# Block products of a latent-attention input stage: order of the last two products, pace of the operands, one rotary step for all latent keys

## The chip, the cores and the metric

The kernel runs on one core of a Trainium2 chip. The core has five engines with a queue of instructions each: TensorE (PE in the profile; PEld is its weight load), VectorE (DVE), ScalarE (ACT), GpSimd (POOL) and SyncE (SP), which issues most DMAs. TensorE writes only to PSUM, which has eight banks of 128 x 512 float32 words; vector and scalar read it, GpSimd doesn't. The metric is the device time in microseconds of one execution. For several executions the median stands.

## The reference

Two layers of a backbone over 1024 latent tokens with 256 context tokens, width 1024. Layer 0 is windowed attention, layer 1 multi-head latent attention, each behind an adaptive normalisation. The change lies at the start of layer 1, where the normalised tokens are multiplied by one input matrix and the result is cut into four parts:

```python
def project(h):
    n = h.shape[1]
    cq, ckv, kr, g = jnp.split(h @ w_in, [B_Q_LORA, B_Q_LORA + B_KV_LORA, B_Q_LORA + B_KV_LORA + B_ROPE], axis=-1)
    q = (rms_norm(cq, q_norm) @ w_uq).reshape(b, n, B_HEADS, B_NOPE + B_ROPE)
    kv = (rms_norm(ckv, kv_norm) @ w_ukv).reshape(b, n, B_HEADS, B_NOPE + B_V)
    return q[..., :B_NOPE], q[..., B_NOPE:], kv[..., :B_NOPE], kr, kv[..., B_NOPE:], g
...
qrx = apply_rope(qrx, cos, sin)
krx = apply_rope(krx, cos, sin)
```

`cq` has 512 columns, `ckv` 256, `kr` 32 and `g` 1024. `ckv` and `kr` are needed for all 1280 tokens, `cq` and `g` for the 1024 latent ones. `kr` of the latent tokens is turned by a rotary step: it is multiplied by a cosine, its halves are swapped and multiplied by a signed sine, and the two are added.

## The kernel before

**Float32 by three products.** A float32 factor is cut into a high part (a cast by ScalarE, line 125) and a low part (what is left, a subtraction by VectorE or GpSimd, line 126); this is `split`. A product of two such factors is three matmuls, lines 130 to 132 (`mm3`). Nearly all matmuls of this stage have these three lines, whatever they belong to.

**The latent tiles.** `kv_tile` multiplies 128 tokens by the 288 columns of `ckv` and `kr` into one of three PSUM banks. It takes the norm of the first 256 columns (`rstd`: a square on ScalarE, line 1025, a scaling on VectorE, line 1026, a power on GpSimd, line 1027), scales them (line 1065) into a ring buffer `e`, and puts the last 32 columns into `krF`, a copy for the two context tiles and a rotary step (`rope`, lines 281, 286 and 291) for the eight latent ones. Two transposes (line 1078), a split and two stores of a tile are kept in a list `pend` and done by `flush` up to two tiles later. Ten tiles are done in the order `order1`. Between them the tokens of later tiles are normalised (`norm_x`, lines 231 to 234) and turned (`turn_h`, lines 245 to 254).

**The block products.** `cq` and `g` are computed by a scheme that makes a two by two block product of seven products instead of eight. The weights are six groups of 256 columns, two of kind `cq` and four of kind `g`; a group's weights are cut into four blocks (`raw(i, j)`), the tokens into two halves of the width and two halves of the sequence. `t_sums` makes the token side, T1 to T4, from sums and differences (lines 1093 to 1102), once for each half of the 512 token pairs. On the weight side `op(n)` makes the operand of product n: A11, A12, A22, and S1 to S4 with the sums in lines 1137, 1139, 1143 and 1151. Each operand is split into a slot of `wslot`, a ring of eight, with its low part on GpSimd. `fetch` loads a group's weights in two halves into a ring of two buffers (line 1118).

`P(n)` is a product of twelve 128 x 512 matmuls. A group has four PSUM banks d, c, a, b. P(1) and P(2) share d, P(6) uses c, P(5) uses b and P(7) uses a. P(4) adds to what P(7) left in a, and P(3) adds to what P(5) left in b. Before that, the result of P(5) or P(7) is read out of the bank by a vector addition (line 1177). The results of P(4) and P(3) are read in line 1185, and P(6)'s in line 1171. `post` then stores a block; for the kind `cq` it also sums squares (`sqacc`, lines 1201 to 1205), and for the kind `g` it applies a gate function (line 1192).

Products of one group run in the order of `todo`: 6, 5, 7, 4, 3, with P(1) and P(2) done ahead or in between. The operands come from one generator, `operands()`, which runs over all groups; after every product one `next(ops)` makes one operand, so that the operands stay eight ahead of the products, and the load of a group stands directly ahead of its first operand. `latent_rms` makes the factor of the `cq` norm from `sqacc`: sixteen small matmuls (line 1210), a scaling and a power (1214, 1215), eight transposes (line 1220) and two copies (line 1221).

**After the groups** `qr_tile` multiplies eight tiles by the rotary part of the query weights, applies `rope`, and leaves four transposes (line 1248) and two stores to `pend`; `flush(2)` does them two tiles later. Later `make_kr` reads `krF`.

Outside the part marked `manual_schedule`, a planner sets the order of the instructions on every engine: it goes by the order of the program and by when it takes an instruction's inputs to be ready. So matmuls of a tile and of a product can stand mixed on TensorE.

Of the kernel before, what the change touches and what calls it, by code (L numbers as in the profile page):

```python
# [60 lines left out]
def kernel(ctx: ExitStack, tc: tile.TileContext, t, out, dbg=None):  # L61
# [990 lines left out]
    def kv_tile(ti):  # L1052
# [13 lines left out]
        kr = krF[:, ti : ti + 1, :]  # L1066
        if ti < 2:
            nc.vector.tensor_copy(kr, shp(ps[:, 256:288], 1, 32))
        else:
            rope(  # L1070
                kr, shp(ps[:, 256:288], 1, 32), cosb[:, ti - 2, :], sinb[:, ti - 2, :], 1, 32,
                shp(e[:, 288:320], 1, 32),
            )
# [13 lines left out]
        pend.append(rest)  # L1087

# [18 lines left out]
    class Group:  # L1107

        def __init__(self, c0, kind, ch, banks):
            self.c0, self.kind, self.ch = c0, kind, ch  # L1110
            self.d, self.c, self.a, self.b = [PB[:, i, :] for i in banks]

        def fetch(self, n=2):
            self.w = []
            for h in range(2):
# [3 lines left out]
                self.w.append(w)  # L1119
# [87 lines left out]
    def latent_rms():  # L1207
# [8 lines left out]
        for h, bank in ((0, 6), (1, 7)):  # L1216
            pt = PB[:, bank, :]
            for i in range(4):
                r = rc[:, 4 * h + i : 4 * h + i + 1].to_broadcast([128, 128])
                nc.tensor.transpose(pt[:, i * 128 : i * 128 + 128], r, ident)  # L1220
            nc.scalar.copy(r_b[h], pt)
# [60 lines left out]
    rest5 = (6, 5, 7, 4, 3)  # L1282
    todo = [(0, (1, 2)), (1, (1, 2))] + [(i, rest5) for i in range(4)]
    todo += [(4, (1, 6, 5, 7, 2, 4, 3)), (5, (1, 6, 2, 5, 7, 4, 3))]

    def operands():
        for i, ns in todo:
            groups[i].fetch(len(ns) // 4 + 1 if len(ns) > 2 else 1)
            for n in ns:
                groups[i].op(n)  # L1290
                yield

    t_rest = []
    ops = operands()
    order1 = [2 * p + j for p in (0, 1, 3, 2, 4) for j in range(2)]
    nx = norm_x(src1(order1[4]), xr, junk)
    for i, ti in enumerate(order1):
# [9 lines left out]
        if i in (1, 5):  # L1307
            g = groups[2 + i // 4]
            g.d = PB[:, 3 + i // 4, :]
            g.fetch(1)  # L1310
# [11 lines left out]
        if i == 7:  # L1322
            t_rest.append(t_sums(xts[2], xts[4], slice(256, 512), xts[2][:, 4:8]))
        if i in (5, 7):
# [3 lines left out]
            if i == 7:  # L1328
                wslot.i = 0
                next(ops)  # L1330
                next(ops)
    flush()
    next(ops)
    next(ops)
    wr = Ring(F, [30, 26], 1024)
    for _ in range(4):
        next(ops)
        if t_rest:
            t_rest.pop(0)()
    for gi, ns in todo:  # L1340
        g = groups[gi]
        last = gi == 5
        for i, n in enumerate(ns):
            g.P(n)
            next(ops, None)
            if gi == 4 and i == 1:
                latent_rms()
# [564 lines left out]
```

## Time and profile before

| | us |
|---|---|
| median of 3 runs | 1595.35 (1591.12 to 1597.8) |
| the profiled execution | 1591.68 |
| its span, first to last instruction | 1590.0 |
| latent tiles begin (about) | 710 |
| block products, all but those among the latent tiles | 780.7 to 917.2 |
| eight query tiles and what follows | 917.2 to 985 |

The profile of the execution, its first two parts cut to the engines that matter here:

```profile
DVE  3878996657777777766633453667677677577354
ACT  4432222377777777768523433455555555545322
POOL 1151212136565555443554462588688688689410
PEclk9999999999999999998989999999999999999999
```

Each of the forty digits is a slice of 39.75 us and gives the busy share in tenths (9 is 90% or more); PEclk is the clock that was granted to TensorE, in tenths of full speed. The stage of the block products runs from slice 20 to the start of slice 24, counted from 1. A wait in a profile's list names the engine and line that waited, what released it, the total in us, the number of times and the longest. A row of the timeline gives start, length, engine, line, operation and tiles, and in brackets how long the engine had been idle and what ended it.

### The profile page before, as it was taken

Reading aid. Unit: us, or ns where it says so; the run is one execution under the profiler, and the core shown is the slowest. Engines: PE = TensorE matmul, PEld = TensorE weight load, DVE = VectorE, ACT = ScalarE, POOL = GpSimd, SP = SyncE. Lnnn points to the kernel's source line nnn. Section 1 sums busy time; section 2 is a strip of 40 time slices with the busy share of each in tenths; the row PEclk is TensorE's granted clock in tenths of the full one; section 3 lists DMA queues with packets and bytes.
Section 4 is the critical chain, followed back from the end, with each engine's and each line's share of the span. In section 5 each row is a group of like instructions: output and inputs, shape, how many; then the busy total and the mean of one; then the engine's idle time right before and its main releaser. Section 6 shows DMA issues by size and latency. Waiting matters only on the chain.

```text
span 1590.0 us, 25744 instructions
## 1 busy us (share of the span) xinstructions
PE 1528.5 (96%) x9190; PEld 1189.0 (75%) x9190; DVE 1040.6 (65%) x1768; ACT 801.4 (50%) x1540; POOL 809.3 (51%) x847
## 2 busy tenths in 40 slices
PE   6999999999999999998889899999999999999998
PEld 4988888886888888877767678666766766766687
DVE  3878996657777777766633453667677677577354
ACT  4432222377777777768523433455555555545322
POOL 1151212136565555443554462588688688689410
PEclk9999999999999999998989999999999999999999
DMA  8357674654343333244443476233232323244251
GB/s 315 112 158 219 199 202 132 199 160 113 94 136 97 94 98 93 81 139 146 115 128 103 148 242 222 87 77 104 67 97 81 86 79 96 67 131 117 69 166 66
DMA packets 160079, 204.01 MB, mean 128 GB/s; under 512 B 14656, under 2 KB 94016, under 8 KB 159952
## 3 DMA queue, kind: packets, MB, share of 16 engines
q1 hardware_dynamic: 158480, 200.48, 42.0%
q10 hardware_dynamic: 1472, 1.90, 0.4%
q8 instruction: 72, 1.18, 0.3%
q14 instruction: 55, 0.45, 0.1%
HBM read 151.46 MB, written 50.87 MB: 127 GB/s over the span
## 4 chain that ended last, share of the span: by engine, by line
PE 72%; DVE 8%; issue 5%; DMA 5%; POOL 5%; ACT 4%; SPq 1%; DVEq 0%; POOLq 0%; ACTq 0%
PE PB L1543 11%; PE PB L130 11%; PE PB L131 10%; PE PB L132 10%; PE PB L1565 8%; PE PB L1506 4%; PE PB L617 4%; PE PB L658 4%; PE PB L648 4%; POOL arena_r L126 2%; DVE arena_f L195 2%; DVE arena_f L515 1%; ACT arena_r L125 1%; PE PB L1514 1%; DMA arena_f<-a_w_in 1%
## 5 line engine op out<-in xcount | busy, mean ns | idle before, releaser
L130 PE MATMUL PB<-arena_r 128*128 128x512 f32 (+2 forms) x990 | 367.5, 373 | 4.4 <-ACT arena_r L419 2.4
L1557 POOL TENSOR_TENSOR arena_f<-arena_f 128x512 f32<-128x512 f32 x252 | 328.0, 1302 | 81.9 <-ACT arena_f L1549 65.1
L131 PE MATMUL PB<-arena_r 128*128 128x512 f32 (+2 forms) x958 | 352.7, 369 | 1.2 <-POOL arena_r L685 0.8
L132 PE MATMUL PB<-arena_r 128*128 128x512 f32 (+2 forms) x926 | 339.1, 367 | 0.0
L126 POOL TENSOR_TENSOR arena_r<-arena_f,arena_r 128x512 fp32r<-128x512 f32 x106 | 148.4, 1412 | 308.1 <-ACT arena_r L125 251.5
L1549 ACT ACTIVATE arena_f<-PB 128x1024 f32<-128x1024 f32 x160 | 164.1, 1027 | 108.7 <-PE PB L1543 69.9
L130 PEld LDWEIGHTS PB<-arena_r 128*128 128x128 f32 x990 | 187.0, 190 | 39.1 <-ACT arena_r L419 4.8
L1508 DVE TENSOR_REDUCE arena_f<-PB 128x1 f32<-128x1024 f32 x128 | 156.0, 1219 | 86.3 <-PE PB L1506 86.2
L131 PEld LDWEIGHTS PB<-arena_r 128*128 128x128 f32 x958 | 182.5, 190 | 30.0 <-DVE arena_r L420 2.3
L132 PEld LDWEIGHTS PB<-arena_r 128*128 128x128 f32 x926 | 176.3, 190 | 28.6 <-issue 1.7
L1543 PE MATMUL PB<-arena_r 64*128 64x512 f32 (+1 forms) x1490 | 194.4, 392 | 0.3 <-ACT arena_f L1549 0.3
L1543 PEld LDWEIGHTS PB<-arena_r 64*128 64x128 f32 (+1 forms) x1490 | 135.6, 185 | 29.2 <-ACT arena_f L1549 1.8
L126 DVE TENSOR_TENSOR arena_r<-PB,arena_r 128x512 fp32r<-128x512 f32 (+1 forms) x171 | 115.7, 684 | 61.0 <-ACT arena_r L125 60.2
L1565 PE MATMUL PB<-arena_f 128*64 128x512 f32 x640 | 144.4, 597 | 0.0
L628 DVE CUSTOM_DVE_ANT_0 arena_f<-PB,arena_f,small 128x640 f32<-128x640 f32 (+2 forms) x176 | 125.1, 722 | 19.3 <-PE PB L617 12.5
L125 ACT CAST arena_r<-arena_f 128x512 fp32r<-128x512 f32 (+1 forms) x139 | 83.2, 618 | 106.8 <-PE PB L132 38.0
L631 ACT ACTIVATE arena_f<-arena_f,small 128x640 f32<-128x640 f32 (+2 forms) x160 | 119.5, 747 | 34.7 <-DVE small L628 32.1
L125 ACT CAST arena_r<-PB 128x512 fp32r<-128x512 f32 (+1 forms) x171 | 98.1, 581 | 46.3 <-PE PB L648 44.1
L617 PE MATMUL PB<-arena_k,arena_r 128*128 128x256 f32 (+1 forms) x576 | 111.2, 308 | 1.5 <-DVE small L628 1.3
L1565 PEld LDWEIGHTS PB<-arena_f 128*64 128x64 f32 x640 | 43.1, 136 | 83.2 <-issue 79.6
L648 PE MATMUL PB<-ident,arena_f 128*128 128x128 f32 x672 | 103.9, 274 | 0.8 <-DVE arena_r L126 0.3
L617 PEld LDWEIGHTS PB<-arena_k,arena_r 128*128 128x128 f32 x576 | 89.2, 188 | 13.9 <-DVE small L628 3.5
(245 smaller groups left out, 2644.1 us busy)
## 6 DMA issues: line engine op xcount, KB each, us to landing
arena_f<-ada_w SPq DMA_DIRECT2D x40, 512.0 KB, 4.8
arena_r<-q_d SPq DMA_DIRECT2D x80, 256.0 KB, 3.7
arena_r<-qn_d SPq DMA_DIRECT2D x64, 256.0 KB, 4.0
arena_r<-qr_d SPq DMA_DIRECT2D x170, 64.0 KB, 3.3
arena_f<-a_w_in SPq DMA_DIRECT2D x40, 256.0 KB, 3.2
g_d<-arena_f SPq DMA_DIRECT2D x32, 256.0 KB, 3.3
q_d<-arena_f SPq DMA_DIRECT2D x64, 128.0 KB, 2.5
qn_d<-arena_f SPq DMA_DIRECT2D x16, 512.0 KB, 3.0
```

The costliest lines, as they stand in the source:

```text
L125: nc.scalar.copy(hi, src)
L126: (lo_eng or nc.vector).tensor_sub(lo, src, hi.bitcast(F32))
L130: nc.tensor.matmul(o, ah, bh, start=first, stop=False, skip_group_check=more)
L131: nc.tensor.matmul(o, al, bh, start=False, stop=False, skip_group_check=more)
L132: nc.tensor.matmul(o, ah, bl, start=False, stop=last, skip_group_check=more)
L617: nc.tensor.matmul(S[:, at : at + n], qT[:, s, hq, :], kT[:, g, k : k + n], start=s == 0, stop=s == 1)
L648: nc.tensor.transpose(pt[:, h, :], self.Ps[h][:, ci * 128 : ci * 128 + 128], ident)
L1508: nc.vector.reduce_max(mx[:, 32 + b : 33 + b], flat, AX.X, negate=True)
L1543: nc.tensor.matmul(S[:, t], k[r, c : c + 128], q[r], start=j == 0, stop=j == 4)
L1549: nc.scalar.activation(E, self.S, AF.Exp)
L1557: eng.tensor_add(self.acc, self.acc, E[:, t])
L1565: nc.tensor.matmul(self.pv[p : p + 64], Vq[:, cs[t], self.h % 4, :], E[:, t], start=i == 0, stop=i == 4)
```

## The change

The last two products of a group change places (6, 5, 7, 3, 4). Each latent tile copies its 32 columns raw into `krF` on ScalarE, and one step, `kr_rope`, turns all eight latent tiles together later. The generator of the operands goes: each group's operands are made during its predecessor's products, two behind a product for the groups up to the fourth and behind the first of the fifth, else one, and as soon as they are all made the load of the group behind is issued. The first two operands of the two `cq` groups are loaded and made during the last two latent tiles, and P(1) of both groups comes ahead of the last tiles' transposes. The sums of the second half of the tokens move behind the latent tiles. `latent_rms` is cut in two, with two products in between, the rows of the second half are loaded one product earlier, and `flush(2)` in the query tiles becomes `flush(3)`.

```diff
@@ kv_tile
-        kr = krF[:, ti : ti + 1, :]
-        if ti < 2:
-            nc.vector.tensor_copy(kr, shp(ps[:, 256:288], 1, 32))
-        else:
-            rope(
-                kr, shp(ps[:, 256:288], 1, 32), cosb[:, ti - 2, :], sinb[:, ti - 2, :], 1, 32,
-                shp(e[:, 288:320], 1, 32),
-            )
+        nc.scalar.copy(krF[:, ti, :], ps[:, 256:288])
...
+    def kr_rope():
+        u = krF[:, 2:10, :]
+        o, tmp = [shp(er.bufs[i], 8, 32) for i in range(2)]
+        nc.vector.tensor_mul(o, u, cosb)
+        uv, sv, tv = [v.rearrange("p h (a b c) -> p h a b c", a=2, b=2) for v in (u, sinb, tmp)]
+        for b in range(2):
+            nc.vector.tensor_mul(tv[:, :, :, b, :], uv[:, :, :, 1 - b, :], sv[:, :, :, b, :])
+        nc.gpsimd.tensor_add(u, o, tmp)
@@ Group
-        def fetch(self, n=2):
-            self.w = []
-            for h in range(2):
+        def fetch(self, halves=(0, 1), n=2):
+            for h in halves:
...
-                self.w.append(w)
+                self.w[h] = w
@@ latent_rms
-    def latent_rms():
+    def latent_rms(step):
+        if step == 3:
+            for h, bank in ((0, 6), (1, 7)):
...
+                nc.scalar.copy(r_b[h], pt)
+            return
@@ the order of the stage
-    rest5 = (6, 5, 7, 4, 3)
-    todo = [(0, (1, 2)), (1, (1, 2))] + [(i, rest5) for i in range(4)]
-    todo += [(4, (1, 6, 5, 7, 2, 4, 3)), (5, (1, 6, 2, 5, 7, 4, 3))]
-
-    def operands():
-        for i, ns in todo:
-            groups[i].fetch(len(ns) // 4 + 1 if len(ns) > 2 else 1)
-            for n in ns:
-                groups[i].op(n)
-                yield
+    todo = [(i, (6, 5, 7, 3, 4)) for i in range(4)]
+    todo += [(4, (1, 6, 5, 7, 2, 3, 4)), (5, (1, 6, 2, 5, 7, 3, 4))]
+
+    def first_op(i, n):
+        groups[i].fetch((n - 1,), 1)
+        groups[i].op(n)
...
-        if i == 7:
-            t_rest.append(t_sums(xts[2], xts[4], slice(256, 512), xts[2][:, 4:8]))
         if i in (5, 7):
             g = groups[2 + i // 7]
             g.P(1)
             g.P(2)
-            if i == 7:
-                wslot.i = 0
-                next(ops)
-                next(ops)
+            wslot.i = 0
+        if i > 7:
+            first_op(0, i - 7)
+            first_op(1, i - 7)
+        if i == 8:
+            groups[0].P(1)
+    groups[1].P(1)
     flush()
-    next(ops)
-    next(ops)
+    t_rest.append(t_sums(xts[2], xts[4], slice(256, 512), xts[2][:, 4:8]))
     wr = Ring(F, [30, 26], 1024)
-    for _ in range(4):
-        next(ops)
-        if t_rest:
-            t_rest.pop(0)()
+    for f in t_rest:
+        f()
+    groups[0].fetch()
+    groups[0].P(2)
+    groups[1].P(2)
+    for n in todo[0][1]:
+        groups[0].op(n)
+    groups[1].fetch()
+    kr_rope()
     for gi, ns in todo:
         g = groups[gi]
         last = gi == 5
+        ops = [] if last else list(todo[gi + 1][1])
         for i, n in enumerate(ns):
             g.P(n)
-            next(ops, None)
-            if gi == 4 and i == 1:
-                latent_rms()
+            for _ in range(2 if gi < 4 or i == 0 else 1):
+                if ops:
+                    groups[gi + 1].op(ops.pop(0))
+                    if not ops and gi < 4:
+                        groups[gi + 2].fetch()
+            if gi == 4 and i in (1, 3):
+                latent_rms(i)
...
-            if last and i == 1:
+            if last and i == 0:
                 rows.append(load_rows(1))
...
     for ti in range(8):
         qr_tile(ti)
-        flush(2)
+        flush(3)
```

More of the change, by code (lines that the diff above doesn't have):

```diff
@@ L1109, in __init__ @@
         def __init__(self, c0, kind, ch, banks):
-            self.c0, self.kind, self.ch = c0, kind, ch
+            self.c0, self.kind, self.ch, self.w = c0, kind, ch, {}
             self.d, self.c, self.a, self.b = [PB[:, i, :] for i in banks]
-        def fetch(self, n=2):
-            self.w = []
-            for h in range(2):
+        def fetch(self, halves=(0, 1), n=2):
+            for h in halves:
                 w = shp(wr.next(), 4, 128 * n)
@@ L1205, in post @@
             nc.gpsimd.tensor_add(sqacc[half], sqacc[half], sq)
-    def latent_rms():
+    def latent_rms(step):
+        if step == 3:
+            for h, bank in ((0, 6), (1, 7)):
+                pt = PB[:, bank, :]
+                for i in range(4):
+                    r = rc[:, 4 * h + i : 4 * h + i + 1].to_broadcast([128, 128])
+                    nc.tensor.transpose(pt[:, i * 128 : i * 128 + 128], r, ident)
+                nc.scalar.copy(r_b[h], pt)
+            return
         ps = PB[:, 6, :]
@@ L1215, in latent_rms @@
         nc.gpsimd.tensor_tensor(rc, rc, mhalf.to_broadcast([128, 8]), ALU.pow)
[L1216 to L1221, printed above, removed]
     def load_rows(h):
@@ L1281 @@
         g.p1 = p1
-    rest5 = (6, 5, 7, 4, 3)
-    todo = [(0, (1, 2)), (1, (1, 2))] + [(i, rest5) for i in range(4)]
-    todo += [(4, (1, 6, 5, 7, 2, 4, 3)), (5, (1, 6, 2, 5, 7, 4, 3))]
-    def operands():
-        for i, ns in todo:
-            groups[i].fetch(len(ns) // 4 + 1 if len(ns) > 2 else 1)
-            for n in ns:
-                groups[i].op(n)
-                yield
+    todo = [(i, (6, 5, 7, 3, 4)) for i in range(4)]
[3 more added lines that the diff above has]
+        groups[i].op(n)
     t_rest = []
-    ops = operands()
     order1 = [2 * p + j for p in (0, 1, 3, 2, 4) for j in range(2)]
@@ L1309 @@
             g.d = PB[:, 3 + i // 4, :]
-            g.fetch(1)
+            g.fetch(n=1)
             g.op(1)
```

## The prediction

> **What bounds the kernel now.** I read the page first: TensorE is busy for 96% of the span, so time can only come out where TensorE stops or runs slowly.
>
> ```profile
> span 1590.0 us, 25744 instructions
> PE 1528.5 (96%) x9190; PEld 1189.0 (75%) x9190; DVE 1040.6 (65%) x1768; ACT 801.4 (50%) x1540; POOL 809.3 (51%) x847
> ```
>
> Then the waits of TensorE alone, from 700 to 930 us, the stretch that the diff touches.
>
> ```profile
> PE PB L130 <- DVE arena_f L1177: 14.1, 5, 4.2
> PE PB L1078 <- DVE arena_f L1065: 4.2, 1, 4.2
> PE PB L245 <- ACT arena_f L249: 2.9, 2, 2.7
> PE PB L245 <- DVE arena_f L234: 2.1, 2, 1.6
> PE PB L131 <- POOL arena_r L126: 1.8, 1, 1.8
> PE PB L1248 <- POOL arena_f L291: 1.6, 1, 1.6
> PE PB L1220 <- POOL small L1215: 1.1, 1, 1.1
> ```
>
> The largest is line 1177, the vector add that reads the result of P(5) or P(7) out of PSUM: 14.1 us in five waits. P(4) accumulates into the bank that P(7) has just filled (`self.a`), so P(4), directly behind P(7), has to wait for that add. Next, busy time by stretches (length, PE, PEld, DVE, ACT, POOL, granted clock, DMA share, GB/s):
>
> ```profile
> 780.70:917.20 136.50, 119.52 (x485) 95.63 (x486) 58.60 (x86) 47.20 (x83) 69.02 (x55) 0.91 0.42 128
> 810.10:815.40 5.30, 5.30 (x13) 4.14 (x14) 0.53 (x1) 1.22 (x2) 1.28 (x1) 0.50 0.51 148
> ```
>
> The first row is the whole stage of block products: 136.5 us at a mean clock of 0.91. The second is 5.3 us behind one of the waits: clock 0.50. So a wait costs twice, once idle and once in slow matmuls. The timeline of TensorE gives both sizes: two rows at full pace, then the first and a late row of each slow stretch.
>
> ```profile
> 798.69 0.39 PE L130 MATMUL PB<-arena_r 128*128 128x512 f32 x1
> 805.49 0.39 PE L130 MATMUL PB<-arena_r 128*128 128x512 f32 x1
> 810.09 0.79 PE L130 MATMUL PB<-arena_k,arena_r 128*128 128x512 f32 x1 [4.21 <-DVE arena_f L1177]
> 814.95 0.63 PE L132 MATMUL PB<-arena_k,arena_r 128*128 128x512 f32 x1
> 828.76 0.50 PE L130 MATMUL PB<-arena_k,arena_r 128*128 128x512 f32 x1 [2.42 <-DVE arena_f L1177]
> 832.33 0.57 PE L130 MATMUL PB<-arena_k,arena_r 128*128 128x512 f32 x1
> 846.99 0.80 PE L130 MATMUL PB<-arena_k,arena_r 128*128 128x512 f32 x1 [2.74 <-DVE arena_f L1177]
> 853.13 0.42 PE L132 MATMUL PB<-arena_r 128*128 128x512 f32 x1
> 911.18 0.79 PE L130 MATMUL PB<-arena_k,arena_r 128*128 128x512 f32 x1 [3.75 <-DVE arena_f L1177]
> 914.71 0.39 PE L132 MATMUL PB<-arena_k,arena_r 128*128 128x512 f32 x1
> ```
>
> From 798.69 to 805.49 lie 30 steps: 6.80/30 = 0.227 us per matmul, so a product of twelve takes 2.72 us. The 38 products of the stage would take 456 x 0.227 = 103.4 us and its small matmuls about 3; the rest of 136.5, about 30 us, is lost. Behind the first gap, 11 steps take 4.86 us where 2.49 would do: 2.4 lost. In the same way the second stretch (9 steps, 3.57 for 2.04) loses 1.5, the third (14 steps, 6.14 for 3.17) 3.0, the fourth (8 steps, 3.53 for 1.81) 1.7. Together 8.6 us of slow pace behind four gaps.
>
> Why is the add late? Vector and SyncE around the first gap, and vector at the last:
>
> ```profile
> 805.03 0.38 SPq L1118 DMA_DIRECT2D arena_f<-b_w_in  x1
> 808.74 0.69 DVE L1137 TENSOR_TENSOR arena_f<-arena_f 128x512 f32<-128x512 f32 x1 [1.77 <-DMA arena_f<-b_w_in]
> 809.35 0.68 DVE L1177 TENSOR_TENSOR arena_f<-PB,arena_f 128x512 f32<-128x512 f32 x1
> 908.64 1.88 DVE L126 TENSOR_TENSOR arena_k<-arena_f,arena_r 128x512 fp32r<-128x512 f32 x3
> 910.45 0.68 DVE L1177 TENSOR_TENSOR arena_f<-PB,arena_f 128x512 f32<-128x512 f32 x1
> ```
>
> The add stands on vector behind L1137, the first operand sum of a coming group, and that waits for a weight load issued only at 805.03. In the last group it stands behind three splits (L126).
>
> **The change, part by part.**
>
> *P(3) before P(4).* P(3) accumulates into P(5)'s bank, whose add ran during P(7); P(4) then finds P(7)'s add 2.72 us old. The four gaps of 4.21, 2.42 and 2.74 us (first three groups) and 0.94 us (fifth, the remainder of 14.1) go in full once the add no longer waits for a load. In the last group the add ended at 911.13, about 3.8 us after P(7), so 1.0 of 3.75 stays. Gained: 14.1 - 1.0 = 13.1 us, and with it 8.6 us of slow pace. A pure swap without the load's cover would still leave P(4) 1.5 us late at the worst gap (4.21 - 2.72).
>
> The Trainium skill, "TensorE: Matmul & The Clock Gate", section "What's actually happening", says that the clock falls to half after an idle window of about 3.4 us. By that rule alone the gaps of 2.42 and 2.74 us would have no slow stretch and the gain would be 4.5 us smaller; the rows show a stretch behind each, so the measurement decides.
>
> *Two operands per product, loads earlier.* The number of operands, loads and splits stays; five operands of a group are now done after three of its predecessor's products, and the load for the group behind is issued then, about two products and one more (8 us) ahead of use. The costs of one load, split and sum, with the places where they met at the start of the stage:
>
> ```profile
> DMA to landing us min/median/max: 2.8/3.8/4.5
> L126 POOL TENSOR_TENSOR arena_r<-arena_f,arena_r 128x512 fp32r<-128x512 f32 x46 | 65.3, 1432 | 73.6 <-ACT arena_r L125 63.6 <-DVE arena_f L1185 8.4 <-DVE arena_f L1177 1.4
> L1205 POOL TENSOR_TENSOR arena_f<-arena_f 128x512 f32<-128x512 f32 x6 | 8.2, 1361 | 0.3 <-ACT arena_f L1204 0.3
> L1151 DVE TENSOR_TENSOR arena_f<-arena_f x6: 691/1763/1774, 789.7 to 883.0; 128x512 f32<-128x512 f32 x6
> 775.74 3.92 POOL L126 TENSOR_TENSOR arena_r<-arena_f,arena_r 128x512 fp32r<-128x512 f32 x2 [1.64 <-ACT arena_r L125]
> 780.20 0.48 DVE L1065 SCALAR_TENSOR_TENSOR arena_f<-PB,small,arena_f 128x256 f32<-128x256 f32 x1 [1.27 <-POOL small L1027]
> 792.01 1.26 POOL L126 TENSOR_TENSOR arena_r<-arena_f,arena_r 128x512 fp32r<-128x512 f32 x1
> L1099 DVE TENSOR_TENSOR arena_r<-arena_f,arena_r x4: 1218/1246/2316, 743.7 to 772.9; 128x1024 fp32r<-128x1024 f32 x4
> ```
>
> A load lands in at most 4.5 us, so 8 us cover it. GpSimd needs 5 x 1.43 + 3 x 1.36 = 11.2 us of a 13.6 us group in the two cq groups: it fits, with 2.4 us of room. In a burst, 2 x 1.43 = 2.87 us per product is a little over 2.72. What it costs the trace of before doesn't show: below nothing if earlier operands also end small waits elsewhere, and nothing is quoted for that; above, a collision lengthens a sum from 0.69 to 1.77 us (L1151), 1.1 us, and if one such collision reached TensorE in each of six groups, 6.5 us. I take 2 us, near the short end, because operands have two products of slack.
>
> The Trainium skill, "SBUF — State Buffer", section "Who interferes with whom", says a vector instruction with two SBUF inputs and a GpSimd instruction that reads SBUF exclude each other for a whole instruction. The 1.77 us of L1151 agree with it; by that rule every one of the six would collide, the 6.5 us above.
>
> *The start of the stage.* Before, the last latent tile's power (L1027) stood on GpSimd behind two splits (775.74, 3.92 us); TensorE waited 4.2 us for line 1065 and lost, as I estimate from the four slow stretches above (1.5 to 3.0 us), some 1.8 us more behind it. Then P(6) waited 1.8 us for the split at 792.01. Now `groups[0].P(1)` and `groups[1].P(1)`, 5.4 us of matmuls, lie ahead of those last transposes and cover the 4.2 us. The second half's sums (`t_sums`: four subtractions, four casts, four splits) move behind the tiles on vector and scalar, out of the way of the norms, but are nearer to P(6). P(6)'s first operand still needs its load, sums and split after the four first operands, so I leave a wait of 2.5 us with its slow pace before P(6). Gained: 4.2 + 1.8 + 1.8 - 2.5 = 5.3 us.
>
> *Rotary in one step.* Rows of before, and the nearest one for the new copy:
>
> ```profile
> L281 DVE TENSOR_TENSOR krF<-PB,arena_f x8: 177/181/184, 730.7 to 783.2; 128x32 f32<-128x32 f32 x8
> L286 DVE TENSOR_TENSOR arena_f<-PB,arena_f 128x16 f32<-128x16 f32 x16 | 2.0, 164 | 0.0
> L291 POOL TENSOR_TENSOR krF<-krF,arena_f x8: 253/908/1222, 731.1 to 783.6; 128x32 f32<-128x32 f32 x8
> L490 ACT COPY small<-PB x18: 144/160/163, 100.6 to 292.9; 128x2 f32<-128x2 f32 x18
> ```
>
> Vector loses 8 x 0.18 + 16 x 0.16 = 4.0 us and GpSimd 8 x 0.91 = 7 us; scalar gets ten copies of 0.16 us or a little more (L490 has 2 columns, they have 32); the one late step has three vector instructions, each under the 0.69 us of a 512-wide one, beside the products, where vector is busy 58.6 of 136.5 us. All lies beside TensorE. In the latent tiles TensorE waits 2.9 + 2.1 us for L249 and L234, partly behind this work: I book nothing, and keep 5 us for the range.
>
> *latent_rms in two steps, flush(3).* The transposes L1220 come two products later, 5.4 us, against a wait of 1.1: gone. The transposes L1248 come one tile (2.7 us) later against 1.6: gone. Together 2.7 us. `load_rows(1)` and its four loads come one product earlier on SyncE; what waits behind them is only stores of finished blocks.
>
> **The sum.** 13.1 + 8.6 + 5.3 + 2.7 - 2 = 27.7 us. The profiled execution took 1591.7 us (span 1590.0 and 1.7 around it), so 1564.0; it was near the fastest of the three runs, whose median 1595.35 is 3.7 above it. I add that: **1567.5 us**. Behind the stage TensorE works on without a gap (first figures: length 40.00, PE busy 40.00), so nothing there gives it back:
>
> ```profile
> 945.00:985.00 40.00, 40.00 (x201) 33.41 (x201) 13.63 (x25) 15.52 (x32) 12.98 (x13) 1.00 0.73 244
> ```
>
> **The rivals.**
>
> *A late start takes most of it.* If `t_sums` begins only behind the last tile's norm, P(6) lacks T2: three subtractions and a split of 1.2 to 2.3 us each (L1099), 5 to 9 us, against two products (5.4 us), so up to 4 us. With the 6.5 us of collisions 10.5 us more are lost, and some 2 of slow pace: saved 15, 1580. For it: GpSimd's small room. Against: the vector engine has gaps earlier, in which the sums may run, as they did before.
>
> *The swap does nothing alone.* The order of each engine is set by a planner; if it kept P(4) first, only the load's cover would help: the gaps shrink to one add, about 0.7 us, five times, without slow pace. Saved about 25, 1570; it's inside the forecast.
>
> *Nothing left at the end.* If the qr stage waits for its own weight loads (b_w_uq), arriving 25 us earlier only moves the wait: within 8 us of before. Against: those loads are released by the same products.
>
> *Slower: operands too late.* The slot ring holds eight operands, ten are wanted, so the fourth and fifth wait for P(6) and P(5) of the running group; the scalar cast that waits for this holds all behind it. If through this a group's last split lands after its fifth product, the next load starts there, and the next P(6) waits load 3.8 + two sums 1.4 + split 1.4 = 6.6 us, with 2.5 us slow pace, at five groups: 45 us, against 31 that today's waits cost: 14 more, 1610. It decides from 5.4 us of lateness on. The 2.4 us of room per group speak against it.
>
> **How the numbers follow.** Forecast 0.62 (1556 to 1576), late start 0.20 (1580), no change 0.10, slower 0.08. Range 1553 to 1586: below, all 14.1 + 8.6 + 7.8 + 2.7 and the 5 us of the latent tiles, 38 us; above, the late start with 6 us more. About 0.5% (8 us) is what a measurement of this kernel can tell from no change; faster by more 0.84, within it 0.09, slower 0.07.
>
> **What would show it.** Right: no wait of TensorE on L1177's add over 1 us, granted clock about 0.98 from 800 to 900 us, a products' stage of about 112 us, no DMA wait ahead of the operand sums. Wrong: a wait over 5 us before P(6) of the first group, waits of TensorE on GpSimd's splits in every group, or a new wait at the qr tiles as long as what was saved.

## The result and the profile after

| | before | after |
|---|---|---|
| median of 5 runs, us | 1593.88 (1589.37 to 1597.8) | 1578.20 (1577.32 to 1581.62) |
| ratio | | 0.9907, 95% interval 0.9883 to 0.9932 |
| the profiled execution and its span, us | 1591.68, 1590.0 | 1577.52, 1575.7 |

The kernel became faster by 15.7 us, or 0.9%. The forecast was 1567.5 with a range of 1553 to 1586: the sign is right, the time lies in the range, and the gain is little more than half of the 27.7 us that the sum had given. The time lies outside the 1556 to 1576 that I had named for the forecast itself, next to the 1580 of the rival of a late start. (1564.0 and 3.7 make 1567.7; the 1567.5 is a slip.) Line numbers shift: 1078 is now 1071, 1118 is 1119, 1137 to 1151 are 1138 to 1152, 1171 is 1172, 1177 is 1178, 1185 is 1186, 1193 is 1194, 1248 is 1251, 1366 is 1374, 1369 is 1377.

The waits of TensorE in the profile after, from 700 to 930 us (what waited, what released it, total us, times, longest):

```profile
PE PB L130 <- ACT arena_r L125: 6.8, 2, 6.1
PE PB L245 <- ACT arena_f L249: 4.5, 2, 3.9
PE PB L1251 <- POOL arena_f L291: 3.5, 1, 3.5
PE PB L130 <- ACT krF L1066: 3.2, 1, 3.2
PE PB L130 <- DVE arena_f L1178: 2.0, 2, 1.3
```

The 14.1 us on line 1177 are 2.0 us on line 1178, and the 4.2 us at the start of the stage are gone from the head of the list. Two waits are new: 6.1 us on a cast, and 3.5 us at a transpose of the query tiles. The 3.2 us for line 1066, in the latent tiles, stand where TensorE had waited 2.9 us for line 1026; the prediction's list of waits leaves that row of before out. The windows after (length, busy time of PE, PEld, DVE, ACT, POOL, granted clock, DMA share, GB/s):

```profile
781.70:900.00 118.30, 109.05 (x485) 88.97 (x484) 65.37 (x85) 50.26 (x89) 68.59 (x53) 0.97 0.50 148
800.00:810.00 10.00, 4.43 (x13) 3.57 (x14) 5.89 (x7) 3.00 (x5) 7.19 (x5) 0.66 0.45 129
900.00:985.00 85.00, 81.48 (x406) 66.73 (x405) 34.30 (x62) 27.50 (x50) 34.29 (x31) 0.96 0.71 225
```

The products' stage has 485 matmuls as before and takes 118.3 us where it took 136.5; the clock in it rose from 0.91 to 0.97. The ten microseconds from 800 hold the new wait: TensorE is busy for 4.43 of them, at a clock of 0.66. The third row is the query tiles and what follows: 81.48 of 85 us busy, the rest idle.

**Where the time went.** For every matmul in a timeline I take the step to the next start and subtract the step of dense work (0.227 us for 512 columns, 0.133 for 288, 0.12 for 256, 0.065 for 128). The sum over a stretch is its loss, idle time and slow clock together. It closes: from 700 to 965 us the loss falls from 58.5 to 44.3, 14.2 us, and the span fell by 14.3.

| loss in us | before | after | forecast of the gain | gain |
|---|---|---|---|---|
| latent tiles (700 to 775) | 19.6 | 22.2 | 0 | -2.6 |
| start of the stage (775 to 795) | 8.5 | 1.1 | 5.3 | 7.4 |
| the products after it, but for the next row | 26.9 | 4.7 | 22.8 | 22.2 |
| before and in P(3) of the first group (795 to 811) | 0 | 7.9 | -2 | -7.9 |
| query tiles | 3.5 | 8.4 | 1.6 | -4.9 |
| sum | 58.5 | 44.3 | 27.7 | 14.2 |

The third row's forecast is 13.1 + 8.6 + 1.1. In the profile before, what was lost between 795 and 811 us stood ahead of P(4) and is counted in the third row; ahead of P(3) nothing was. So the waits that the change was to end did end, as far as they were counted; two new ones took 12.8 us back.

**The first new wait.** VectorE in the profile after, around it, with rows of ScalarE, GpSimd and TensorE:

```profile
791.76 0.62 ACT L125 CAST arena_r<-arena_f 128x512 fp32r<-128x512 f32 x1 [0.55 <-DVE arena_f L1152]
794.29 1.29 POOL L126 TENSOR_TENSOR arena_r<-arena_f,arena_r 128x512 fp32r<-128x512 f32 x1
797.29 1.76 DVE L1144 TENSOR_TENSOR arena_f<-arena_f 128x512 f32<-128x512 f32 x1 [0.85 <-POOL krF L1089]
798.98 0.68 DVE L1172 TENSOR_TENSOR arena_f<-PB,arena_f 128x512 f32<-128x512 f32 x1
799.58 0.67 DVE L1138 TENSOR_TENSOR arena_f<-arena_f 128x512 f32<-128x512 f32 x1
800.28 1.64 DVE L1140 TENSOR_TENSOR arena_f<-arena_f 128x512 f32<-128x512 f32 x1
803.08 1.74 DVE L1152 TENSOR_TENSOR arena_f<-arena_f 128x512 f32<-128x512 f32 x1 [1.16 <-POOL arena_r L126]
804.74 0.68 DVE L1178 TENSOR_TENSOR arena_f<-PB,arena_f 128x512 f32<-128x512 f32 x1
799.78 7.41 POOL L126 TENSOR_TENSOR arena_r<-arena_f,arena_r 128x512 fp32r<-128x512 f32 x5 [1.28 <-ACT arena_r L125]
805.57 0.77 PE L130 MATMUL PB<-arena_r 128*128 128x512 f32 x1 [6.09 <-ACT arena_r L125]
```

The profile puts TensorE's wait down to a cast (line 125), since the second group's fourth operand was cast just then. But the matmul at 805.57 opens P(3) of the first group, whose own operand had been cast by 792.4 (first row) and its low part made by 795.6 (second row). P(3) adds to the bank that P(5) filled, and the add that reads it out (line 1178) ran at 804.74. Ahead of it on VectorE stand the four operand sums of the second group (lines 1144, 1138, 1140, 1152), and the last of them waits 1.16 us for a split on GpSimd, which has five in a row from 799.78 to 807.19. The add's own inputs were there at 799.66, when line 1172 had ended. The wait of before, a vector add behind an operand sum that isn't ready, came back, at another bank and with another thing to wait for: a split where it had been a load.

This order isn't new. In the profile before, too, the four operand sums of the second group stand ahead of P(5)'s add; here are the last of them, the add, and the first matmul of P(3):

```profile
800.85 1.76 DVE L1151 TENSOR_TENSOR arena_f<-arena_f 128x512 f32<-128x512 f32 x1 [1.26 <-POOL arena_r L126]
802.53 0.68 DVE L1177 TENSOR_TENSOR arena_f<-PB,arena_f 128x512 f32<-128x512 f32 x1
804.13 0.39 PE L130 MATMUL PB<-arena_r 128*128 128x512 f32 x1
```

(From 798.69, where P(5) begins, to 805.49 TensorE makes 31 matmuls in a row. P(5) and P(7) have twenty-four; the other seven are P(3)'s, which the planner had put ahead of P(4), and five more follow behind P(4).) The add had ended at 803.21, 0.9 us before P(3) began, so nothing waited. In the profile after, P(7) is through 4.8 us earlier (its last matmul begins at 799.09, not at 803.91), and the add begins 2.2 us later. 4.8 + 2.2 - 0.9 makes the 6.1 us. Thus a good part of what the start of the stage had gained was lost again here: TensorE came sooner, the add didn't.

**The second new wait.** The timeline of SyncE, VectorE and TensorE at the first query tiles, and then, from the view of line 1377 alone, its time from issue to landing:

```profile
899.17 0.99 SPq L1374 DMA_DIRECT2D arena_f<-b_w_uq  x2
900.25 0.46 SPq L1377 DMA_DIRECT2D arena_k<-ckv_d  x1
901.03 0.34 SPq L1194 DMA_DIRECT2D g_d<-arena_f  x1
901.47 0.38 SPq L1377 DMA_DIRECT2D arena_k<-ckv_d  x1
909.70 0.69 DVE L281 TENSOR_TENSOR arena_f<-PB,arena_f 128x512 f32<-128x512 f32 x1 [4.82 <-DMA g_d<-arena_f]
912.45 1.11 PE L1251 MATMUL PB<-ident,arena_f 128*128 128x128 f32 x4 [3.52 <-POOL arena_f L291]
```

```profile
DMA to landing us min/median/max: 8.6/8.6/8.6
```

TensorE's transposes at 912.45 wait for the last addition (line 291) of the rotary step of the first query tile. VectorE does this step second, at 909.70, and it writes to the first buffer of its ring, `ev = Ring(F, [34, 45, 47, 6], 512)`. In that buffer lay the block of the last product, and its store (line 1194, 901.03) was issued behind two small loads (line 1374) and between the two halves of a large one (line 1377). The first half took 8.6 us; of the second the trace has no landing.

The buffer isn't new. The blocks take theirs from the ring `ov` in the order of the program, as often per group whichever product is last, so before the change the last block, then P(3)'s, lay in the same one. SyncE and VectorE there:

```profile
915.60 0.37 SPq L1369 DMA_DIRECT2D arena_k<-ckv_d  x1
917.21 1.69 SPq L1193 DMA_DIRECT2D g_d<-arena_f  x2
922.64 1.37 DVE L281 TENSOR_TENSOR arena_f<-PB,arena_f 128x512 f32<-128x512 f32 x2 [3.69 <-PE PB L132]
```

The second of the two stores, issued at 918.58, had landed when the second of the two steps began at 923.32, so it took at most 4.7 us. It stood 3.0 us behind the half load, and the two small loads stood behind it. What the change altered is the order on SyncE's queue: three loads are now issued within the 1.9 us ahead of the last store.

### The profile page after: what moved, and what is told of

It is laid out like the page before. It is cut to its first block, busy times and chain, and to the rows that moved or that the text cites. A ratio compares the mean times of both kernels' runs of the same rounds, so it can differ in the third digit from the quotient of the medians.

```text
span 1575.7 us, 25723 instructions
## 1 busy us (share of the span) xinstructions
PE 1523.3 (97%) x9190; PEld 1187.6 (75%) x9190; DVE 1045.0 (66%) x1745; ACT 803.0 (51%) x1550; POOL 804.5 (51%) x840
## 5 line engine op out<-in xcount | busy, mean ns | idle before, releaser
L1557 ACT ACTIVATE arena_f<-PB 128x1024 f32<-128x1024 f32 x160 | 164.1, 1026 | 109.4 <-PE PB L1551 69.1
L617 PEld LDWEIGHTS PB<-arena_k,arena_r 128*128 128x128 f32 x576 | 89.5, 188 | 14.1 <-DVE small L628 3.5
```

The source lines that it names most:

```text
L617: nc.tensor.matmul(S[:, at : at + n], qT[:, s, hq, :], kT[:, g, k : k + n], start=s == 0, stop=s == 1)
L1557: nc.scalar.activation(E, self.S, AF.Exp)
```

## The experiments

"The changed kernel" is the one after; each edit is against it unless it says otherwise. Ratios are to the kernel before, with a 95% interval.

**The swap alone**, in the kernel before:

```diff
-    rest5 = (6, 5, 7, 4, 3)
+    rest5 = (6, 5, 7, 3, 4)
-    todo += [(4, (1, 6, 5, 7, 2, 4, 3)), (5, (1, 6, 2, 5, 7, 4, 3))]
+    todo += [(4, (1, 6, 5, 7, 2, 3, 4)), (5, (1, 6, 2, 5, 7, 3, 4))]
```

`todo` orders the operands as well, so those of the two products change places too.

> The kernel before with only the last two products of each group exchanged. Theory: the swap takes P(4) away from the add behind it, but the vector queue still stands behind a weight load, so each gap shrinks by at most one product (2.72 us) and the slow pace behind the gaps of 2.4 to 4.2 us goes: 14.1 us of waits become 2 to 4, 8.6 us of slow pace become 0 to 2, ratio about 0.988. Rival, the load's cover is what counts: the operand sums that wait for the load now hold the other adds as well, TensorE waits as long one product later, ratio 0.996 to 1.0.

Measured: 1580.69 us, ratio 0.9925 (0.9910 to 0.9940), 11.7 us below the 1592.43 of before on the same chip, between what the theory and the rival had named. Its wait on line 1177 (us, times, longest), and VectorE at the longest one:

```profile
PE PB L130 <- DVE arena_f L1177: 5.2, 3, 3.4
```

```profile
821.38 1.74 DVE L1143 TENSOR_TENSOR arena_f<-arena_f 128x512 f32<-128x512 f32 x1 [3.72 <-POOL arena_r L126]
823.04 1.46 DVE L1177 TENSOR_TENSOR arena_f<-PB,arena_f 128x512 f32<-128x512 f32 x2
```

The swap by itself took 8.9 of the 14.1 us, and before P(4) only 1.8 us of waiting are left (the 3.4 us stand before a P(3)). The products explain about half of these 12.3 us: in the first three groups and the last, six or seven matmuls of P(3) had stood ahead of P(4) before, so that the swap puts only the other five or six there, 1.1 to 1.4 us a time, and about 6 us with the 0.9 of the fifth group. The other half is VectorE's order. P(7)'s add, which stood behind the sum that waits for the load (808.74 and 809.35 in the prediction's rows), now stands ahead of it:

```profile
808.60 0.68 DVE L1177 TENSOR_TENSOR arena_f<-PB,arena_f 128x512 f32<-128x512 f32 x1
811.86 0.69 DVE L1137 TENSOR_TENSOR arena_f<-arena_f 128x512 f32<-128x512 f32 x1 [2.58 <-DMA arena_f<-b_w_in]
```

It is the same in the changed kernel (807.83 and 809.63), and there as here VectorE waits for the loads as before or longer: 7.0 us in four waits before, 10.1 with the swap alone, 7.7 in the changed kernel. What the swap left is an add behind an operand sum (line 1143) that waits 3.72 us for GpSimd: the mechanism of the 6.1 us wait is there without the rest of the change.

**Everything but the swap:**

```diff
-    todo = [(i, (6, 5, 7, 3, 4)) for i in range(4)]
-    todo += [(4, (1, 6, 5, 7, 2, 3, 4)), (5, (1, 6, 2, 5, 7, 3, 4))]
+    todo = [(i, (6, 5, 7, 4, 3)) for i in range(4)]
+    todo += [(4, (1, 6, 5, 7, 2, 4, 3)), (5, (1, 6, 2, 5, 7, 4, 3))]
```

> The changed kernel with P(4) before P(3) as it was; paced operands, late sums, one rotary step and the rest stay. Theory: with no load ahead of it the add of P(7) costs TensorE only its own 0.7 to 0.8 us per group, five times, without slow pace: 4 us slower than the changed kernel, ratio to before about 0.993. Rival, the swap is the main part: the waits on that add come back at 2 to 4 us each with slow pace, 15 us or more, ratio 1.0 or above.

Measured: 1582.46 us, ratio 0.9936 (0.9919 to 0.9952).

```profile
PE PB L130 <- DVE arena_f L1178: 9.3, 3, 4.0
PE PB L130 <- ACT arena_r L125: 7.3, 1, 7.3
```

The time is the one that the theory named, but not for its reason: the waits on the add came back as in the rival, up to 4.0 us, and in the second and third group the add stands behind the sum that waits for the load again (822.96 and 824.30 in the second). Alone, the swap gives 11.7 us and the rest 10.0; together they give 15.7. They don't add, as both take from the same five waits. A wait on the cast stands here too, with 7.3 us, ahead of seven matmuls of P(3) that the planner puts directly behind P(7) in this kernel as well; so it isn't the swap that brings it. TensorE's wait at the query tiles is gone: the last two stores (909.72 and 911.12) stand ahead of the two small loads (911.53 and 912.08) again. With the swap alone they don't, and TensorE waits 2.8 us: that wait is the swap's.

**The rotary step's scratch elsewhere.** `kr_rope` at 795.62 had waited 3.89 us for GpSimd, because its scratch lies over the buffers of the operand sums:

```diff
-        o, tmp = [shp(er.bufs[i], 8, 32) for i in range(2)]
+        o, tmp = [shp(r_b[i], 8, 32) for i in range(2)]
```

> The changed kernel with the two scratch tiles of the rotary step in the space that later holds the norm's factor, not in the first two buffers of the latent tiles, which share their words with the ring of operand sums. Theory: the rotary step waits for GpSimd's splits of the first group's sums (3.9 us of vector idle at 791.7), and the next sums wait for it, so P(5)'s add comes at 804.7 and TensorE stands 6.1 us and runs slowly for about 1.7: with the scratch moved this goes, 6 to 8 us faster than the changed kernel, ratio to before about 0.986. Rival: GpSimd's backlog of five splits (7.4 us from 799.8) is the bound, two operands per product being too many for it; then the wait moves by less than 2 us.

Measured: 1578.18 us, ratio 0.9908 (0.9891 to 0.9925): no change. VectorE in it:

```profile
794.25 0.69 DVE L1144 TENSOR_TENSOR arena_f<-arena_f 128x512 f32<-128x512 f32 x1 [2.89 <-POOL arena_r L126]
...
800.22 1.74 DVE L1152 TENSOR_TENSOR arena_f<-arena_f 128x512 f32<-128x512 f32 x1 [2.38 <-POOL arena_r L126]
801.88 0.68 DVE L1178 TENSOR_TENSOR arena_f<-PB,arena_f 128x512 f32<-128x512 f32 x1
```

The add is 2.9 us earlier on the clock, but the sums' own waits for GpSimd grew to 2.89 and 2.38 us and TensorE still waits 5.4 us. This theory fell.

**The query tiles' ring begins with another buffer:**

```diff
-    ev = Ring(F, [34, 45, 47, 6], 512)
+    ev = Ring(F, [45, 47, 6, 34], 512)
```

> The changed kernel with the four buffers of the query tiles taken in another order, so that the one which holds the last stored block comes fourth and not first. Theory: the first query tile waits for the store of that block, issued at 901.0 behind a load of 1.25 MB that lands 8.6 us after its issue; vector stands 4.8 us and TensorE 3.5 us with slow pace: with the order changed the wait goes, 4 to 6 us faster than the changed kernel, ratio to before about 0.988. Rival: the query weights or GpSimd's five splits before its first rotary add (898.0 to 905.9) are late; then nothing changes by more than 1 us.

Measured: 1573.76 us, ratio 0.9879 (0.9861 to 0.9898), 4.4 us below the changed kernel's median; the intervals overlap, but the slowest of its four runs (1575.33) is below the fastest of the changed kernel's five (1577.32). The loss in the query tiles fell from 8.4 to 3.4 us. The store lands no sooner, but the tile that now waits for it is the fourth, which has time:

```profile
910.67 0.69 DVE L281 TENSOR_TENSOR arena_f<-PB,arena_f 128x512 f32<-128x512 f32 x1 [2.67 <-DMA g_d<-arena_f]
```

**Five buffers for the operand sums instead of three:**

```diff
-    sr = Ring(F, [8, 10, 12], 512)
+    sr = Ring(F, [8, 10, 12, 18, 20], 512)
```

> The changed kernel with five buffers instead of three in the ring of operand sums. Theory, after the scratch tiles turned out not to be the cause: on vector the second group's sums stand ahead of P(5)'s add, each sum needs a buffer that GpSimd still reads for a split, and GpSimd is behind (five splits, 7 us, from 797 to 804); with two more buffers the sums don't wait, the add comes in time, and the 6.1 us wait and its slow pace go: 5 to 8 us faster than the changed kernel, ratio to before about 0.987. Rival, GpSimd's rate itself is the bound: the operands are late whatever the buffers, the wait moves to a split one or two products later and at most 2 us are gained.

Measured: 1577.63 us, ratio 0.9911 (0.9889 to 0.9933): no change that can be told. The loss from 795 to 811 fell from 7.9 to 4.6 us, and the waits on line 1178 rose from 2.0 us in two to 7.2 in five. With five buffers VectorE hardly waits for GpSimd any more, from 785 to 905 us 5.8 us in three waits instead of 19.3 in eleven. Its waits for the weight loads grew in their place, from 7.7 us in four to 21.8 in seven.

**The copy of the 32 columns on VectorE.** In the changed kernel ScalarE waited 8.9 us in four for line 1065 at its copies into `krF`, which read the bank that VectorE is scaling.

```diff
-        nc.scalar.copy(krF[:, ti, :], ps[:, 256:288])
+        nc.vector.tensor_copy(krF[:, ti, :], ps[:, 256:288])
```

> The changed kernel with the copies of the 32 key columns on vector instead of scalar. Theory: on scalar each copy waits behind vector's scaling of the same PSUM bank (8.9 us of idle time in four waits, 4.0 the longest), and scalar holds the casts and the turned tokens behind it, so the latent tiles lost 2.4 us against before: on vector, where the scaling stands directly ahead of it, this goes, 1 to 3 us faster than the changed kernel. Rival: scalar's idle time is covered, the 2.4 us are the arrangement of that execution; no change, within 1.5 us.

Measured: 1581.79 us, ratio 0.9936 (0.9913 to 0.9958): not faster. A wait of 3.3 us for line 1026 took the place of the 3.2 us for the copy, in the same place, and the 4.7 us for line 249 stayed. The copy on ScalarE costs nothing that could be had back this way.

**The rotary step alone**, in the kernel before, with `kr_rope` behind the groups:

```diff
+        nc.scalar.copy(krF[:, ti, :], ps[:, 256:288])
...
     fetch1(4, nc.vector)
+    kr_rope()
```

> The kernel before with only the rotary change: raw copies on scalar in the latent tiles and one step for all eight tiles behind the six groups. Theory: it saves nothing on TensorE and holds scalar at each copy, 0 to 3 us slower than before, ratio 1.000 to 1.002. Rival: vector loses 4 us and GpSimd 7 us of work in the tiles, and the norms behind them come earlier: 2 to 5 us faster, ratio 0.997 or less.

Measured: 1587.36 us in ten runs, ratio 0.9972 (0.9959 to 0.9985): 3.8 us below the 1591.16 of before, as the rival had it. The loss at the start of the stage fell from 8.5 to 4.4 us, and the 4.2 us wait for the last tile's scaling went; at the same transposes TensorE waits 1.3 us for a split (line 126). So the edit that I had booked at nothing gave, by itself, over half of the 7.4 us at the start.

**The second half's token sums back at their old place:**

```diff
+        if i == 7:
+            t_rest.append(t_sums(xts[2], xts[4], slice(256, 512), xts[2][:, 4:8]))
...
     flush()
-    t_rest.append(t_sums(xts[2], xts[4], slice(256, 512), xts[2][:, 4:8]))
```

> The changed kernel with the sums of the second half of the tokens back at their place among the latent tiles; the early P(1), the paced operands and the rest stay. Theory: the two P(1) cover the last tile's norm, and the planner did the sums in vector's gaps in either case, so nothing changes by more than 1.5 us. Rival: the sums ahead of the norms are what made the last transposes late by 4.2 us, and the wait returns in part: 2 to 5 us slower than the changed kernel.

Measured: 1580.25 us, ratio 0.9936 (0.9911 to 0.9960). The loss at the start stays at 0.8 us and the 6.1 us wait is the same. Where the token sums stand doesn't set the start; the 2 us by which this one is slower lie within the intervals.

**One operand per product in the first three groups** (`range(1 if gi < 3 else 2 if gi < 4 or i == 0 else 1)`) needed no run: the planner puts out the very same order on all five engines. The pace that the diff writes isn't what sets the order of the operands; the planner takes each sum as soon as it reckons its inputs to be there.

**Less work on GpSimd.** In the two `cq` groups the operand S1 is split on VectorE:

```diff
-                self.S1 = self.put(self.s1)
+                self.S1 = self.put(self.s1, nc.vector if self.kind == "cq" else None)
```

> The changed kernel, but in the two cq groups the low part of operand S1 is subtracted on VectorE instead of GpSimd. Theory (GpSimd's rate holds the vector queue: the fourth sum of the second group waits for the split of S1 on GpSimd and stands ahead of P(5)'s add, and the third sum waits for the first group's last split): with one split of four less on GpSimd in each of the two groups the 6.1 us wait of TensorE before P(3) of the first group falls to 1 to 4 us, and its loss of 7.8 us with the slow pace to 2 to 5 us; time about 3 to 5 us below the changed kernel, ratio to the kernel before 0.9875 to 0.9890. Rival (vector is as loaded as GpSimd there, and a split of 0.7 to 1.8 us in its own queue ahead of P(5)'s add costs what the wait for GpSimd did): wait 5 to 7 us as it was, ratio 0.990 to 0.992.

Measured: 1579.21 us, ratio 0.9923 (0.9903 to 0.9943): no faster. The loss from 795 to 811 fell to 3.6 us, as the theory had it. But one group further on VectorE and TensorE read

```profile
820.16 1.73 DVE L1144 TENSOR_TENSOR arena_f<-arena_f 128x512 f32<-128x512 f32 x1 [3.69 <-POOL arena_r L126]
821.82 1.46 DVE L1178 TENSOR_TENSOR arena_f<-PB,arena_f 128x512 f32<-128x512 f32 x2
```

```profile
822.64 0.68 PE L130 MATMUL PB<-arena_r 128*128 128x512 f32 x1 [4.96 <-DVE arena_f L1178]
```

which is the pair of rows of the swap alone: a sum that waits for GpSimd, with P(5)'s add behind it. What the theory said of its place held; what it said of the whole did not, since the time was lost again in the next group.

**Three edits together**, the ring, the scratch and the split of S1:

> The changed kernel with three things altered: the query tiles' ring ends with the buffer of the last product's block instead of beginning with it, the rotary step's scratch lies in the buffers of the cq norm's factor, and S1 of the cq groups is split on VectorE. Theory (the waits are separate, so their gains add): the query tiles give 4.4 us as they did alone, the operand part 3 to 5 us more; about 1570, ratio to the kernel before 0.9845 to 0.9870. Rival (the split on vector gives nothing): the query tiles' gain alone, ratio 0.9870 to 0.9890.

Measured: 1571.25 us, ratio 0.9878 (0.9864 to 0.9893), the same as the ring alone. The gains don't add.

**flush(2) again**, with the ring changed:

```diff
-        flush(3)
+        flush(2)
```

> The changed kernel with the query tiles' ring ending with the last product's block, and flush(2) in place of flush(3) in the query tiles. Theory (with the wait for the store gone, the tile's rotary step takes longer than two tiles give it, so flush(3) is worth the 1.6 us that I booked): TensorE waits 1.5 to 3 us for line 291 or 126 at the tiles' transposes. Rival (without the store two tiles are enough): no such wait over 0.5 us, and flush(3) is worth nothing.

One run: 1573.88 us, and TensorE waits 1.1 us once at line 1251; with `flush(3)` and the same ring it waits 1.1 us once there too. The size was missed by both, the reading is the rival's: `flush(3)` is worth nothing.

**VectorE held to the order of the program** in the groups, with the ring changed:

```diff
+    with tc.manual_schedule(engines={mybir.EngineType.DVE}):
     for gi, ns in todo:
```

(with the loop indented under it.)

> The changed kernel with the query tiles' ring ending with the last product's block, and with VectorE's queue held to the order of the program in the six groups (the planner keeps the order of the other engines): P(5)'s add then stands ahead of the third and fourth sum of the next group, the fourth sum still ahead of P(7)'s add. Theory (the planner's order on vector, with sums that wait for GpSimd ahead of P(5)'s add, makes the 6.1 us wait and its slow pace): the stage's waits for the add and the cast fall from 9.5 us to under 3 us, the time 5 to 9 us below the same ring with the planner's order, ratio to the kernel before 0.982 to 0.985. Rival (the sums are on time only because the planner takes them early; in program order the operands come late, and TensorE waits for casts and splits at each group's first products): waits for ACT L125 or POOL L126 of 1 us or more in three or more groups, ratio 0.987 or above.

Measured: 1570.56 us, ratio 0.9881 (0.9861 to 0.9900). VectorE and TensorE at the place of the 6.1 us wait:

```profile
795.17 0.68 DVE L1172 TENSOR_TENSOR arena_f<-PB,arena_f 128x512 f32<-128x512 f32 x1
796.10 1.76 DVE L1138 TENSOR_TENSOR arena_f<-arena_f 128x512 f32<-128x512 f32 x1 [0.24 <-POOL krF L1089]
797.89 0.69 DVE L1140 TENSOR_TENSOR arena_f<-arena_f 128x512 f32<-128x512 f32 x1
798.50 0.68 DVE L1178 TENSOR_TENSOR arena_f<-PB,arena_f 128x512 f32<-128x512 f32 x1
799.10 1.31 DVE L1144 TENSOR_TENSOR arena_f<-arena_f 128x512 f32<-128x512 f32 x1
800.34 1.79 DVE L1152 TENSOR_TENSOR arena_f<-arena_f 128x512 f32<-128x512 f32 x1
```

```profile
799.33 0.47 PE L130 MATMUL PB<-arena_r 128*128 128x512 f32 x1 [1.06 <-ACT arena_r L125]
798.59 7.17 POOL L126 TENSOR_TENSOR arena_r<-arena_f,arena_r 128x512 fp32r<-128x512 f32 x5 [1.28 <-ACT arena_r L125]
```

and the windows behind it and at the end of the stage:

```profile
805.00:850.00 45.00, 45.00 (x200) 37.27 (x199) 23.23 (x28) 17.89 (x29) 33.37 (x24) 1.00 0.56 161
885.00:900.00 15.00, 10.14 (x30) 6.60 (x30) 10.84 (x11) 7.41 (x15) 10.89 (x9) 0.77 0.71 220
```

P(5)'s add now stands ahead of the third and fourth sum (1144, 1152) and the wait is 1.06 us; the 45 us after it are dense at full clock, although GpSimd makes five splits in a row as before (7.17 us, and 7.41 in the changed kernel). With the rows of the changed kernel, where the add could have run at 799.66 and ran at 804.74, that shows the cause: the order on VectorE. It isn't the only thing that differs, as the planner set the other engines anew around it (behind its row at 796, line 1206 on GpSimd next comes at 805.73, with the ring alone at 813.29). The loss from 795 to 885 is 3.2 us, where the ring alone lost 11.0. But the last group pays: there the program's order puts the scaling of the `cq` rows (line 1235) and its splits ahead, and from 885 to 899 8.6 us are lost. The whole is no faster than the ring alone, within the intervals: at this place the theory held, by the time the rival did. An order that mends both places would, as I estimate from these stretches, lie some 8 us below the ring alone (11.0 less 3.2); it wasn't tried.

## Why the prediction was right or wrong

**The gaps behind P(7) and their slow pace: right in size, for other reasons than mine.** I had 13.1 + 8.6 us, and 1.1 for the transposes of `latent_rms`; the stretch lost 22.2 us less. But "P(4), directly behind P(7)" isn't what the rows show: six or seven matmuls of P(3) stood between them in four of the five gaps, so that the swap had less to put there than the 2.72 us that I counted. Nor do the operand sums wait less for their loads. The rest of the gaps in the first three groups went because P(7)'s add came to stand ahead of those sums on VectorE, an order that I hadn't looked at. In the last group I had left 1.0 us of waiting; 1.28 stayed. With the six matmuls that already stood ahead of P(4) there, my own reckoning would have left 2.4, so this fit is luck.

**"I take 2 us, near the short end, because operands have two products of slack": this step failed.** It cost 7.9 us. I counted how many operands fall to a product and how far ahead of use they lie, which says when an operand must be ready. What mattered was what an early operand sum holds up: it stands on VectorE ahead of the add that frees P(5)'s bank for P(3). That add had 0.9 us of slack before, not two products. TensorE came to P(3) 4.8 us sooner, and I had booked the gain at the start and the cost of the operands as if they had nothing to do with each other. I had named the collisions of GpSimd's small room as a rival, at 6.5 us spread over six groups. The size was close; it fell in one place, by an order on a queue and not by lengthened sums. The time, too, is close to that of another rival, the late start, whose wait before P(6) never came. The pace of two per product had no part in it, since one per product gives the same order.

The sums beside the splits did lengthen: lines 1140 and 1152 took 1.64 and 1.74 us against 0.67 for line 1138 a moment earlier. The Trainium skill, "SBUF — State Buffer", section "Who interferes with whom", by which a two-input vector instruction and a GpSimd instruction that reads SBUF exclude each other, agrees with these rows. The last experiment has the same long sums (1.76 and 1.79 us) and no wait over 1.1 us at this place, so the lengthening alone wasn't what cost the time.

**The start of the stage: right in sum, wrong in its parts.** 7.4 us came where 5.3 were booked. I had left 2.5 us for a wait before P(6); there was none. And the wait of 4.2 us went mostly through the rotary step (3.8 us by itself, 4.1 of loss at this place), for which I had booked nothing; what the two P(1) put in between do without it wasn't run. I had read the last tile's power as held up by two splits on GpSimd alone and overlooked that each latent tile's rotary step stood on the same queues.

**"The transposes L1248 come one tile (2.7 us) later against 1.6: gone": this failed too.** A wait of 3.5 us stood there instead of none, 6.5 us on the wrong side with its slow pace. I had followed the order of the products through the banks, but not through SyncE's queue and the buffers: the last store came to stand directly behind three loads, and the next stage begins with the buffer that this store empties. With the ring turned, `flush(3)` itself gave nothing.

**The latent tiles** lost 2.6 us more in the profile after. The eleven other kernels with the new rotary step lost 19.6 to 21.0 us there, 20.4 in the mean, against 19.6 before; so most of the 2.6 lies within the spread between these kernels. No cause was shown for the rest.

**The checks that I had named.** "No wait on the add over 1 us": by the list the longest is 1.3, but the 6.1 us are a wait on that add too, so this check spoke against the forecast, and the list alone would have hidden it. "Clock about 0.98 from 800 to 900": 0.97 over the stage. "A stage of about 112 us": 118.3; the first new wait is as long as the 6.3 us between. "No DMA wait ahead of the operand sums": there are four, 7.7 us in all, as many as before; this check failed. "Wrong: a wait over 5 us before P(6) of the first group": none came there, but the 6.1 us stand before P(3) of that group. "Wrong: a new wait at the qr tiles as long as what was saved": a new one did come there, much shorter than that.

## What to carry to other kernels

When a step is moved, follow three things and not only two: the bank or buffer that it needs, the queue of the engine that frees this bank, and the queue of the store that must land before the buffer of its result is free. Ask also what slack the next meeting with another engine has: time won ahead of it beyond that slack is lost there again. A wait that the profile puts down to one engine may belong to another: ask what the waiting instruction needs, and look for the row that ended last among those. With a planner, look at the order that it puts out before a price is put on the order that the program writes.

## What the runs showed of the hardware

From 850 to 930 us in the profile before, the trace has the landing of one store of a block (line 1193):

```profile
DMA to landing us min/median/max: 3.5/3.5/3.5
```

In the profile after, the one issued at 901.03, 0.8 us behind the first half of the large load, which took 8.6 us, was waited for until 909.70, 8.7 us. I had not expected a small store (256 KB) to take as long as the large transfer (1280 KB) that it was issued beside. The Trainium skill, "DMA: Bandwidth & Descriptors", section "Queues, rings and completion order", says that all DMAs of one issuing engine share one ring on each DMA engine and that their descriptors are taken in the order of the ring; both rows stand on SyncE's queue, and the store's 8.7 us beside the load's 8.6 us agree with that. In seven other kernels with this order of load and store the load took 7.5 to 9.6 us, and VectorE was let go 0.7 to 0.8 us behind its landing in each of them, as in the profile after (0.8). No run here moved the store ahead of the load.
